# Attention scores of two key groups as 64-row products in the two halves of the array, in three steps per chunk

## The chip, the core and the metric

The kernel runs on one core of one Trainium2 chip. The metric is the device time of one execution in microseconds; the median of several runs is compared. The engines are PE (TensorE, the matrix array, with PEld for its weight loads), DVE (VectorE), ACT (ScalarE), POOL (GpSimd) and SP (SyncE, which issues most DMAs). Matrix products write into PSUM, which has eight banks here: four in a pool `acc` and four in a pool `mx`.

## The reference

One inference step of a decoder of two layers, for a prompt of 512 tokens and 8 samples of 4 new tokens (544 tokens in all, width 1024). A layer is a SwiGLU feed-forward half-step, a mixer and a second half-step; the mixer is four heads of a gated delta rule beside a sliding-window attention with 8 query heads of 64, in two groups that share a key and a value head each. The part that the change touches is the attention of the prompt, in chunks of 128 tokens: every query sees its own chunk and the one before, 128 keys back, with a learned sink in the softmax.

```python
s = jnp.einsum('bnqhgd,bnkhd->bnhgqk', q, k).astype(jnp.float32) * (SWA_HEAD_DIM ** -0.5)
s = jnp.where(allowed[None, :, None, None], s, -jnp.inf)
sink = jnp.broadcast_to(sinks.astype(jnp.float32)[None, None, :, :, None, None], s.shape[:-1] + (1,))
p = jax.nn.softmax(jnp.concatenate([s, sink], axis=-1), axis=-1)[..., :-1]
return jnp.einsum('bnhgqk,bnkhd->bnqhgd', p.astype(v.dtype), v)
```

## The kernel before

Tokens lie along the free dimension and features on the 128 partitions. The dense products (the feed-forwards and the projections into and out of the mixer) are in `mm3`, line 588: every product is three, with weights and activations split into high and low parts (`whi`, `wlo`, `xh`, `xl`), on 256 or 288 tokens at a time, and they write `ps_d` in the pool `acc`. Everything else of the mixer is written as generators, called streams here: `attention`, `sample_attention`, `inverse`, `chain` and others. After each dense product `mm3` calls `pump`, which runs the ready stream of the best rank (`PRIO`) up to its next `yield`. A `yield 0` gives the turn back to the dense products for one product; a `yield` of a number of steps puts the stream to sleep for so many. All streams share the four banks of `mx`, in turn: the next `mx` tile waits until the bank that was taken longest ago is free. SBUF tiles of 128 x 512 come from a pool of 64 slots.

`ORDER` sets the order of the heads' projections in the mixer. At its "|" `drain` pumps the streams without dense products until the transforms of all heads (`T`, `QK`, `VI` in the trace) are there. A scheduler then sets the final order on each engine from the program so written.

The attention's steps on the streams' clock are eight blocks of scores, i = 2n + gg for chunk n and group gg. `sq[hh]` holds the queries of head hh of group 0 in partitions 0 to 63 and of group 1 in 64 to 127; `kfe` holds the keys in the same way. For a product over all 128 rows, the kernel keeps a copy of the keys for each group with zeros in the other half, `kz` (lines 1342 to 1346). `scores(i)` makes four products with the chunk before (`ps_sp`, line 1359, not for n = 0) and four with its own (`ps_sc`, line 1366), each with a `yield 0` behind it, so that dense products come between; ACT copies `ps_sp` into the tile `A`, DVE writes `ps_sc` over it where the mask allows (line 1368), and `softmax` follows on DVE, ACT (the exps, line 1332) and POOL. `turn(i)` transposes the block on PE (`ps_pt`, line 86), and `values(n)` multiplies both groups with the values (`ps_av`, lines 1392 and 1396). `LAG` sets how many blocks lie between them. `sample_attention` uses `kz` once more, for the samples' own keys (`ps_nw`, line 1447).

Of the kernel before, what the change touches and what calls it, by code (L numbers as in the profile page):

```python
# [39 lines left out]
def kernel(  # L40
# [23 lines left out]
    def slot(shape, name, dt=F32):  # L64
        return slot_p.tile(shape, dt, tag="s", name=name)
# [7 lines left out]
    def mx(shape, name):  # L73
        return mx_p.tile(shape, F32, tag="mx", name=name)
# [4 lines left out]
    def bc(ap, axis, n):  # L79
        a = ap.unsqueeze(axis)  # L80
        s = list(a.shape)
        s[axis] = n
        return a.to_broadcast(s)
# [589 lines left out]
    def mixer(l, p, norm, nxt, pre):  # L673
# [663 lines left out]
        def attention():  # L1337
            yield from ready("kv", "sq")
            kfe, vt, sq = W["kfe"], W["vt"], W["sq"]

            oswa.extend(sq)
            kz = [slot([P, NTOK], "kz") for _ in range(2)]
            for gg in range(2):
                gp = slice(64 * gg, 64 * gg + 64)
                pool.memset(kz[gg], 0.0)
                act.copy(out=kz[gg][gp], in_=kfe[gp])
            W["kz"] = kz
            F["kz"] = 1
            W.pop("kfe")
            A, PT = {}, {}  # L1350

            def scores(i):
                n, gg = divmod(i, 2)
                qs = slice(n * P, (n + 1) * P)
                a = slot([P, 4, P], "A")
                if n:
                    ps = mx([P, 4, P], "ps_sp")
                    for hh in range(4):
                        pe.matmul(ps[:, hh], sq[hh][:, qs], kz[gg][:, (n - 1) * P:n * P], start=True, stop=True)  # L1359
                        yield 0  # L1360
                    act.copy(out=a, in_=ps)
                else:
                    pool.memset(a, NEG)
                ps = mx([P, 4, P], "ps_sc")
                for hh in range(4):
                    pe.matmul(ps[:, hh], sq[hh][:, qs], kz[gg][:, qs], start=True, stop=True)  # L1366
                    yield 0
                dve.copy_predicated(out=a, mask=bc(M["lower"].bitcast(U32), 1, 4), data=ps)
                softmax(a, p["sink"][:, 4 * gg:4 * gg + 4])
                A[i] = a  # L1370

            def turn(i):
                n = i // 2
                a = A.pop(i)
                ps = mx([P, 4, P], "ps_pt")
                for hh in range(4):
                    transpose(ps[:, hh], a[:, hh])
                    yield 0
                pc = slot([P, 4, P], "pc")
                dve.tensor_tensor(out=pc, in0=ps, in1=bc(upper, 1, 4), op=ALU.mult)  # L1380
                pp = None
                if n:
                    pp = slot([P, 4, P], "pp")
                    dve.tensor_tensor(out=pp, in0=ps, in1=bc(M["slower"], 1, 4), op=ALU.mult)
                PT[i] = pc, pp

            def values(n):

                po = mx([P, 4, P], "ps_av")
                gs = [(slice(64 * gg, 64 * gg + 64), PT.pop(2 * n + gg)) for gg in range(2)]  # L1390
                for gp, (pc, pp) in gs:
                    pe.matmul(po[gp], vt[:, n, gp], pc, start=True, stop=(n == 0))  # L1392
                    yield 0
                for gp, (pc, pp) in gs:
                    if n:
                        pe.matmul(po[gp], vt[:, n - 1, gp], pp, start=False, stop=True)
                        yield 0
                for hh in range(4):
                    act.copy(out=oswa[hh][:, n * P:(n + 1) * P], in_=po[:, hh])

            la, lb = LAG["turn"], LAG["turn"] + LAG["values"]
            for i in range(8 + lb):
                if 0 <= i - lb and (i - lb) % 2:
                    yield from values((i - lb) // 2)
                if 0 <= i - la < 8:
                    yield from turn(i - la)
                if i < 8:
                    yield from scores(i)
                yield LAG["attn"]
            F["attn"] = 1  # L1410

        def sample_attention():


            yield from ready("kv", "sq", "kz")
            kvs, sq, kz = W["kvs"], W["sq"], W["kz"]
            kct = [slot([P, 4, P], "kct") for _ in range(2)]
            for i in range(2):
                kc = slot([P, 4, P], "kc")
# [24 lines left out]
                act.copy(out=sT[gg].rearrange("p (s c) -> p s c", c=16), in_=ps[:, :, gg])  # L1444
            for gg in range(2):
                ps = mx([P, NS], "ps_nw")
                pe.matmul(ps, qz[:, gg].rearrange("p s c -> p (s c)"), kz[gg][:, NP:NTOK], start=True, stop=True)
                yield 0
                nw = sm("nw", (P, 4, 8), 2)
                dve.tensor_tensor(out=nw, in0=ps.rearrange("p (s t) -> p t s", t=4), in1=bc(M["own_s"], 1, 4), op=ALU.mult)  # L1450
                nk[gg] = sm("nk", (P, 4), 2)
                dve.tensor_reduce(out=nk[gg], in_=nw, axis=AX.X, op=ALU.add)
                yield LAG["t"]
# [252 lines left out]
```

## Time and profile before

| what | value |
|---|---|
| median of 3 runs | 2275.59 us (2273.31 to 2281.57) |
| the profiled execution | 2276.84 us, with a span of 2275.1 us in the trace |
| PE busy | 2245.3 us (99% of the span) |
| PEld busy | 2206.3 us (97%) |
| DVE busy | 1246.7 us (55%) |
| ACT busy | 759.4 us (33%) |
| POOL busy | 258.5 us (11%) |
| mean granted clock of PE | 0.981 of full |

An engine's busy time is the sum of the stretches in which it carries out an instruction; overlapping products count once. A product of two fp32 tiles appears as two passes, so the trace counts twice as many as the program. Successive products overlap in the records, so their period, the difference of two starts, tells what one costs, not its own duration. The granted clock is the share of TensorE's full clock that it was allowed.

### The profile page before, as it was taken

How to read it: one execution, taken by the hardware profiler on the slowest of the kernel's cores; microseconds unless marked ns; L12 is line 12 of the kernel's file. 1: busy time of each engine (PE TensorE's matmuls, PEld its weight loads, DVE VectorE, ACT ScalarE, POOL GpSimd, SP SyncE). 2: the span in 40 equal slices, each digit the busy share in tenths (PEclk: the TensorE clock that was granted, in tenths of full speed). 3: DMA queues.
4: the chain of work that ended last, by engine and by line, in shares of the span. 5: the costliest groups of instructions: out<-in, count | busy, mean ns of one | idle time of the engine just before them, and what ended most of it. 6: DMA issues, size and time to landing. Idle time of an engine off the chain costs nothing.

```text
span 2275.1 us, 41968 instructions
## 1 busy us (share of the span) xinstructions
PE 2245.3 (99%) x17639; PEld 2206.3 (97%) x17639; DVE 1246.7 (55%) x2435; ACT 759.4 (33%) x1479; POOL 258.5 (11%) x356
## 2 busy tenths in 40 slices
PE   8999999999999999999999999999999999999998
PEld 7999999999989999999999999999998999999998
DVE  5535435668658553444554353456776675444346
ACT  4222222444544421222432222234344444222123
POOL 6000000235112000000100000013431120000002
PEclk9999999999989999999999999999997999999999
DMA  4332323452212433323222323234421235223224
GB/s 133 88 90 84 91 86 116 121 127 66 81 64 70 140 103 87 91 84 91 86 85 87 91 84 93 84 116 101 112 76 48 77 88 159 84 87 90 84 84 123
DMA packets 416800, 213.48 MB, mean 94 GB/s; under 512 B 39954, under 2 KB 410898, under 8 KB 416580
## 3 DMA queue, kind: packets, MB, share of 16 engines
q1 hardware_dynamic: 414248, 208.88, 32.2%
q8 instruction: 139, 2.28, 0.4%
q10 hardware_dynamic: 1628, 1.32, 0.2%
q0 software_dynamic: 736, 0.61, 0.1%
q14 instruction: 49, 0.40, 0.1%
HBM read 196.07 MB, written 16.73 MB: 94 GB/s over the span
## 4 chain that ended last, share of the span: by engine, by line
PE 91%; DVE 5%; DMA 1%; ACT 1%; issue 1%; POOL 0%; SPq 0%; DVEq 0%; POOLq 0%; ACTq 0%
PE ps_d L588 83%; DVE wlo L531 1%; DVE xl L312 1%; PE ps_x L1174 1%; PE ps_Z L1005 1%; PE ps_av L1392 1%; PE ps_sc L1366 1%; DVE cacc L825 0%; PE ps_u L1127 0%; PE ps_Y L995 0%; PE ps_sp L1359 0%; DMA raw<-in_ffn_w_gate_dram 0%; PE ps_rb L402 0%; PE ps_Tt L86 0%; DVE x L1596 0%
## 5 line engine op out<-in xcount | busy, mean ns | idle before, releaser
L588 PE MATMUL ps_d<-xl,whi 128*128 128x256 f32 (+1 forms) x3520 | 1029.6, 293 | 2.7 <-DVE xl L312 2.6
L588 PE MATMUL ps_d<-xh,whi 128*128 128x256 f32 (+1 forms) x3520 | 1029.2, 293 | 1.8 <-DVE cin L806 1.6
L588 PE MATMUL ps_d<-xh,wlo 128*128 128x256 f32 (+1 forms) x3520 | 1026.2, 292 | 0.0
L529 ACT CAST whi<-raw 128x1024 fp32r<-128x1024 f32 (+1 forms) x340 | 347.4, 1022 | 1159.4 <-PE ps_d L588 776.5
L588 PEld LDWEIGHTS ps_d<-xh,whi 128*128 128x128 f32 x3520 | 673.1, 191 | 8.8 <-issue 2.9
L588 PEld LDWEIGHTS ps_d<-xl,whi 128*128 128x128 f32 x3520 | 673.2, 191 | 5.4 <-DVE xl L312 3.7
L588 PEld LDWEIGHTS ps_d<-xh,wlo 128*128 128x128 f32 x3520 | 672.7, 191 | 2.6 <-issue 2.4
L531 DVE TENSOR_TENSOR wlo<-raw,whi 128x1024 fp32r<-128x1024 f32 (+1 forms) x340 | 408.1, 1201 | 112.5 <-ACT whi L529 111.3
L588 PE MATMUL ps_d<-hh,wlo 128*128 128x288 f32 (+1 forms) x1408 | 405.1, 289 | 0.0
L588 PE MATMUL ps_d<-hl,whi 128*128 128x288 f32 (+1 forms) x1408 | 405.1, 289 | 0.0
L588 PE MATMUL ps_d<-hh,whi 128*128 128x256 f32 (+1 forms) x1408 | 403.2, 289 | 0.0
L588 PEld LDWEIGHTS ps_d<-hl,whi 128*128 128x128 f32 x1408 | 266.9, 190 | 0.0
L588 PEld LDWEIGHTS ps_d<-hh,wlo 128*128 128x128 f32 x1408 | 266.7, 190 | 0.0
L588 PEld LDWEIGHTS ps_d<-hh,whi 128*128 128x128 f32 x1408 | 265.6, 190 | 0.1
L639 DVE SCALAR_TENSOR_TENSOR x<-ps_d,x 128x256 f32<-128x256 f32 (+1 forms) x192 | 83.3, 439 | 240.5 <-PE ps_d L588 240.1
L608 DVE TENSOR_TENSOR g<-ps_d,rb 128x256 f32<-128x256 f32 (+1 forms) x176 | 77.0, 438 | 235.0 <-PE ps_d L588 215.7
L608 DVE TENSOR_TENSOR u<-ps_d,rb 128x256 f32<-128x256 f32 (+1 forms) x176 | 77.5, 441 | 226.2 <-PE ps_d L588 226.2
L381 POOL TENSOR_TENSOR sq<-sq 128x544 f32<-128x544 f32 x34 | 52.6, 1546 | 1216.9 <-DVE wlo L531 1066.6
L588 PE MATMUL ps_d<-oh,whi 128*128 128x288 f32 (+1 forms) x256 | 73.7, 294 | 1.1 <-DVE x L1596 0.8
L588 PE MATMUL ps_d<-ol,whi 128*128 128x256 f32 (+1 forms) x256 | 74.4, 292 | 0.0
L588 PE MATMUL ps_d<-oh,wlo 128*128 128x256 f32 (+1 forms) x256 | 74.4, 292 | 0.0
L630 ACT CAST hh<-th 128x544 fp32r<-128x544 f32 x88 | 57.0, 647 | 37.2 <-DVE th L627 37.2
(414 smaller groups left out, 2066.2 us busy)
## 6 DMA issues: line engine op xcount, KB each, us to landing
raw<-in_ffn_w_gate_dram SPq DMA_DIRECT2D x88, 512.0 KB
raw<-in_ffn_w_up_dram SPq DMA_DIRECT2D x88, 512.0 KB
raw<-in_ffn_w_down_dram SPq DMA_DIRECT2D x64, 512.0 KB
raw<-in_w_in_dram SPq DMA_DIRECT2D x36, 512.0 KB
raw<-in_ffn_w_down_dram SPq DMA_DIRECT2D x40, 384.0 KB
S<-in_state_gdn_dram SPq DMA_DIRECT2D x32, 256.0 KB
xd<-x SPq DMA_DIRECT2D x16, 272.0 KB
x<-xd SPq DMA_DIRECT2D x16, 272.0 KB
```

The source lines that it names most:

```text
L312: dve.scalar_tensor_tensor(out=lo[:, s], in0=v, scalar=w, in1=h.bitcast(F32)[:, s], op0=ALU.mult, op1=ALU.subtract)
L381: eng.tensor_tensor(out=self.sq, in0=self.sq, in1=s2, op=ALU.add)
L529: act.copy(out=hi[:, 0:kn], in_=v)
L531: dve.tensor_tensor(out=lo[:, 0:kn], in0=v, in1=hi.bitcast(F32)[:, 0:kn], op=ALU.subtract)
L588: pe.matmul(ps, a[:, k], b, start=(k == 0 and a is hi and b is rh), stop=(k == kn - 1 and a is lo))
L608: when(norm, lambda: dve.tensor_tensor(out=dst[:, o:o + n], in0=ps, in1=norm.rb[:, o:o + n], op=ALU.mult))
L630: act.copy(out=a, in_=th)
L639: dve.scalar_tensor_tensor(out=xv, in0=ps, scalar=0.25, in1=xv, op0=ALU.mult, op1=ALU.add)
L1005: pe.matmul(ps[:, q], Tt[q // 4][:, q % 4], Y[:, q], start=True, stop=True)
L1174: pe.matmul(ps[:, :, r0:r0 + 4], ss[s // 4][:, s % 4], kqs[:, :, 32 * h + r0:32 * h + r0 + 4], start=True, stop=True)
L1366: pe.matmul(ps[:, hh], sq[hh][:, qs], kz[gg][:, qs], start=True, stop=True)
L1392: pe.matmul(po[gp], vt[:, n, gp], pc, start=True, stop=(n == 0))
```

## The change

The scores of both groups of a chunk are made in one step. The zero-padded keys are gone: each product reads 64 partitions of `sq` and of `kfe`, group 0 in the upper half of the array's rows, group 1 in the lower, in turn, into a bank for each group and part: `ps_sp` and `ps_sc` take all four banks of `mx` at once. There is no `yield` between the products. The loop has three steps a chunk (values of chunk n − 2, scores of chunk n, turns of chunk n − 1) with a sleep of `LAG["attn"]` behind each, in place of one block for each of 8 + 4 steps. `kfe` is kept to the end of the attention, and the samples' own keys are read from it.

```diff
--- before.py
+++ after.py
@@ -1339,35 +1339,29 @@
             kfe, vt, sq = W["kfe"], W["vt"], W["sq"]
 
             oswa.extend(sq)
-            kz = [slot([P, NTOK], "kz") for _ in range(2)]
-            for gg in range(2):
-                gp = slice(64 * gg, 64 * gg + 64)
-                pool.memset(kz[gg], 0.0)
-                act.copy(out=kz[gg][gp], in_=kfe[gp])
-            W["kz"] = kz
-            F["kz"] = 1
-            W.pop("kfe")
             A, PT = {}, {}
 
-            def scores(i):
-                n, gg = divmod(i, 2)
+            def scores(n):
+
                 qs = slice(n * P, (n + 1) * P)
-                a = slot([P, 4, P], "A")
-                if n:
-                    ps = mx([P, 4, P], "ps_sp")
+                parts = ("ps_sp", "ps_sc") if n else ("ps_sc",)
+                ps = {(name, gg): mx([P, 4, P], name) for name in parts for gg in range(2)}
+                for name in parts:
+                    ks = slice(qs.start - P, qs.start) if name == "ps_sp" else qs
                     for hh in range(4):
-                        pe.matmul(ps[:, hh], sq[hh][:, qs], kz[gg][:, (n - 1) * P:n * P], start=True, stop=True)
-                        yield 0
-                    act.copy(out=a, in_=ps)
-                else:
-                    pool.memset(a, NEG)
-                ps = mx([P, 4, P], "ps_sc")
-                for hh in range(4):
-                    pe.matmul(ps[:, hh], sq[hh][:, qs], kz[gg][:, qs], start=True, stop=True)
-                    yield 0
-                dve.copy_predicated(out=a, mask=bc(M["lower"].bitcast(U32), 1, 4), data=ps)
-                softmax(a, p["sink"][:, 4 * gg:4 * gg + 4])
-                A[i] = a
+                        for gg in range(2):
+                            gp = slice(64 * gg, 64 * gg + 64)
+                            pe.matmul(ps[name, gg][:, hh], sq[hh][gp, qs], kfe[gp, ks], start=True, stop=True)
+                for gg in range(2):
+                    a = slot([P, 4, P], "A")
+                    if n:
+                        act.copy(out=a, in_=ps["ps_sp", gg])
+                    else:
+                        pool.memset(a, NEG)
+                    dve.copy_predicated(out=a, mask=bc(M["lower"].bitcast(U32), 1, 4), data=ps["ps_sc", gg])
+                    softmax(a, p["sink"][:, 4 * gg:4 * gg + 4])
+                    A[2 * n + gg] = a
+                yield 0
 
             def turn(i):
                 n = i // 2
@@ -1398,22 +1392,25 @@
                 for hh in range(4):
                     act.copy(out=oswa[hh][:, n * P:(n + 1) * P], in_=po[:, hh])
 
-            la, lb = LAG["turn"], LAG["turn"] + LAG["values"]
-            for i in range(8 + lb):
-                if 0 <= i - lb and (i - lb) % 2:
-                    yield from values((i - lb) // 2)
-                if 0 <= i - la < 8:
-                    yield from turn(i - la)
-                if i < 8:
-                    yield from scores(i)
-                yield LAG["attn"]
+            for n in range(6):
+                if n >= 2:
+                    yield from values(n - 2)
+                    yield LAG["attn"]
+                if n < 4:
+                    yield from scores(n)
+                    yield LAG["attn"]
+                if 1 <= n < 5:
+                    for gg in range(2):
+                        yield from turn(2 * n - 2 + gg)
+                    yield LAG["attn"]
+            W.pop("kfe")
             F["attn"] = 1
 
         def sample_attention():
 
 
-            yield from ready("kv", "sq", "kz")
-            kvs, sq, kz = W["kvs"], W["sq"], W["kz"]
+            yield from ready("kv", "sq")
+            kvs, sq, kfe = W["kvs"], W["sq"], W["kfe"]
             kct = [slot([P, 4, P], "kct") for _ in range(2)]
             for i in range(2):
                 kc = slot([P, 4, P], "kc")
@@ -1444,7 +1441,7 @@
                 act.copy(out=sT[gg].rearrange("p (s c) -> p s c", c=16), in_=ps[:, :, gg])
             for gg in range(2):
                 ps = mx([P, NS], "ps_nw")
-                pe.matmul(ps, qz[:, gg].rearrange("p s c -> p (s c)"), kz[gg][:, NP:NTOK], start=True, stop=True)
+                pe.matmul(ps, qz[:, gg].rearrange("p s c -> p (s c)"), kfe[:, NP:NTOK], start=True, stop=True)
                 yield 0
                 nw = sm("nw", (P, 4, 8), 2)
                 dve.tensor_tensor(out=nw, in0=ps.rearrange("p (s t) -> p t s", t=4), in1=bc(M["own_s"], 1, 4), op=ALU.mult)
```

The scheduler's order shows what becomes of it. The first place is the scores of chunk 2 in the first layer, on PE. Before (one block of chunk 2; the next block looks alike):

```order
L1359 MATMUL ps_sp<-kz,sqt 128x128
L588 MATMUL ps_d<-xh,whi 128x256
L1359 MATMUL ps_sp<-kz,sqt 128x128
L588 MATMUL ps_d<-xl,whi 128x256
L1359 MATMUL ps_sp<-kz,sqt 128x128
L588 MATMUL ps_d<-xh,wlo 128x256
L1359 MATMUL ps_sp<-kz,sqt 128x128
L588 MATMUL ps_d<-xh,whi 128x256
L1366 MATMUL ps_sc<-kz,sqt 128x128
L588 MATMUL ps_d<-xl,whi 128x256
L1366 MATMUL ps_sc<-kz,sqt 128x128
L588 MATMUL ps_d<-xh,wlo 128x256
```

After, the end of the same chunk's 16 products, behind eight `ps_sp` in turn between the groups (`ps_sp_6074` and `ps_sc_6076` are group 1, `ps_sc_6075` is group 0):

```order
L1354 MATMUL ps_sp_6074<-kfe_5096,sqt_5592 128x128
L588 MATMUL ps_d_6067<-xh_4303,wlo_5867 128x288
L1354 MATMUL ps_sc_6075<-kfe_5096,sqt_5345 128x128
L1354 MATMUL ps_sc_6075<-kfe_5096,sqt_5474 128x128
L1354 MATMUL ps_sc_6075<-kfe_5096,sqt_5533 128x128
L1354 MATMUL ps_sc_6075<-kfe_5096,sqt_5592 128x128
L588 MATMUL ps_d_6067<-xh_4359,whi_5866 128x288
L588 MATMUL ps_d_6067<-xl_4360,whi_5866 128x288
L588 MATMUL ps_d_6067<-xh_4359,wlo_5867 128x288
L1354 MATMUL ps_sc_6076<-kfe_5096,sqt_5345 128x128
L1354 MATMUL ps_sc_6076<-kfe_5096,sqt_5474 128x128
L1354 MATMUL ps_sc_6076<-kfe_5096,sqt_5533 128x128
```

Single products between dense ones have become runs; the two groups' `ps_sp` stand in turn, but their `ps_sc` stand apart, four of group 0 and four of group 1, with dense products between.

The second place is the scores of chunk 3, the last, on PE. Before, the last block's scores (of group 1) stand in the drain, each part in a run, with the products of the delta rule around them:

```order
L1392 MATMUL ps_av<-pc,vt 64x512 x2
L1396 MATMUL ps_av<-pp,vt 64x512 x2
L86 MATMUL ps_pt<-ident,A 128x128 x4
L1359 MATMUL ps_sp<-kz,sqt 128x128 x4
L1366 MATMUL ps_sc<-kz,sqt 128x128 x4
L1174 MATMUL ps_x_6919<-kqs,S_6540 128x2x4 x4
L1174 MATMUL ps_x_6919<-kqs,S_6542 128x2x4 x4
```

After, both groups' scores of chunk 3 stand ahead of the drain, among dense products (`ps_sp_6700` is group 0, `ps_sp_6701` group 1; the first 12 of 29 rows that go on in this way):

```order
L1354 MATMUL ps_sp_6700<-kfe_5096,sqt_5345 128x128
L588 MATMUL ps_d_7209<-xl_4304,whi_6660 128x256
L588 MATMUL ps_d_7209<-xh_4303,wlo_6661 128x256
L1354 MATMUL ps_sp_6700<-kfe_5096,sqt_5474 128x128
L588 MATMUL ps_d_7209<-xh_4359,whi_6660 128x256
L588 MATMUL ps_d_7209<-xl_4360,whi_6660 128x256
L1354 MATMUL ps_sp_6701<-kfe_5096,sqt_5345 128x128
L1354 MATMUL ps_sp_6701<-kfe_5096,sqt_5474 128x128
L1354 MATMUL ps_sp_6700<-kfe_5096,sqt_5533 128x128
L588 MATMUL ps_d_7209<-xh_4359,wlo_6661 128x256
L1354 MATMUL ps_sp_6701<-kfe_5096,sqt_5533 128x128
L588 MATMUL ps_d_7209<-xh_4415,whi_6660 128x256
```

The 16 products of this chunk are no longer in runs: 12 pieces of one to three products, with one or two dense ones between.

The third place is the end of the drain in the first layer, on PE (`ps_Z` belongs to the inverse, `ps_x` and `ps_u` to the samples' delta rule). Before:

```order
L1042 MATMUL ps_Z<-Tt,Y 64x64 x6
L86 MATMUL ps_n_7193<-ident,NT_7133 128x128
L86 MATMUL ps_pt<-ident,A 128x128 x4
L1174 MATMUL ps_x_7215<-kqs,S_7055 128x2x4 x4
L1174 MATMUL ps_x_7215<-kqs,S_7057 128x2x4 x4
L1174 MATMUL ps_x_7252<-kqs,S_7059 128x2x4 x2
L1127 MATMUL ps_u<-VI,Tt 128x128 x4
L1174 MATMUL ps_x_7252<-kqs,S_7059 128x2x4 x2
L1174 MATMUL ps_x_7252<-kqs,S_7061 128x2x4 x4
L1222 MATMUL ps_y_7319<-T_7196,NT_7133 128x128
L1392 MATMUL ps_av<-pc,vt 64x512 x2
L1396 MATMUL ps_av<-pp,vt 64x512 x2
```

After:

```order
L86 MATMUL ps_kd<-ident,kf 128x128 x4
L1042 MATMUL ps_Z<-Tt,Y 64x64 x6
L86 MATMUL ps_n_7216<-ident,NT_7158 128x128
L1174 MATMUL ps_x_7236<-kqs,S_7084 128x2x4 x4
L1174 MATMUL ps_x_7236<-kqs,S_7086 128x2x4 x4
L588 MATMUL ps_d<-xh,whi 128x256
L588 MATMUL ps_d<-xl,whi 128x256
```

Behind the last `ps_Z` the transposes of `A`, half of the `ps_x` and the last `ps_av` are gone from the drain's end; they stand earlier, or among later dense products.

## Rows read from the trace of the kernel before

**Rows 1.** Page, part 1: busy us, share of the span, instructions.

```profile
PE 2245.3 (99%) x17639; PEld 2206.3 (97%) x17639; DVE 1246.7 (55%) x2435; ACT 759.4 (33%) x1479; POOL 258.5 (11%) x356
```

**Rows 2.** Windows: length, busy us of each engine, clock, DMA share, GB/s.

```profile
500.00:530.00 30.00, 30.00 (x250) 30.00 (x250) 23.38 (x70) 13.13 (x41) 10.31 (x18) 1.00 0.45 106
530.00:560.00 30.00, 30.00 (x224) 29.96 (x223) 27.83 (x59) 14.65 (x42) 15.78 (x16) 0.86 0.27 72
```

**Rows 3.** Tile view of kz: duration min/median/max in ns, first and last start.

```profile
L1366 PE MATMUL ps_sc<-kz,sqt x128: 270/275/275, 504.9 to 1729.3; 128*128 128x128 f32 x128
...
L1359 PE MATMUL ps_sp<-kz,sqt x96: 271/275/275, 514.8 to 1728.4; 128*128 128x128 f32 x96
...
L1345 POOL MEMSET kz<- x4: 541/548/550, 494.8 to 1612.3; 128x544 f32 x4
L1346 ACT COPY kz<-kfe x4: 642/643/644, 499.0 to 1615.3; 64x544 f32<-64x544 f32 x4
```

**Rows 4.** Timeline of PE, four scores in a row: start, us, operation.

```profile
504.78 0.28 PE L588 MATMUL ps_d<-xh,whi 128*128 128x256 f32 x1
504.90 1.06 PE L1366 MATMUL ps_sc<-kz,sqt 128*128 128x128 f32 x8
505.71 0.36 PE L588 MATMUL ps_d<-xl,whi 128*128 128x256 f32 x1
505.91 0.28 PE L588 MATMUL ps_d<-xh,wlo 128*128 128x256 f32 x1
```

**Rows 5.** Timeline of PE, single scores between dense products.

```profile
509.33 0.30 PE L588 MATMUL ps_d<-xh,wlo 128*128 128x288 f32 x1
509.46 0.38 PE L1366 MATMUL ps_sc<-kz,sqt 128*128 128x128 f32 x2
...
509.82 0.38 PE L1366 MATMUL ps_sc<-kz,sqt 128*128 128x128 f32 x2
```

**Rows 6.** Timeline of PE, four products of 32 rows.

```profile
751.99 0.29 PE L588 MATMUL ps_d<-xh,wlo 128*128 128x288 f32 x1
752.21 1.14 PE L1283 MATMUL ps_s<-um,kds 32*128 32x512 f32 x8
753.28 0.38 PE L588 MATMUL ps_d<-xh,whi 128*128 128x256 f32 x1
753.50 0.28 PE L588 MATMUL ps_d<-xl,whi 128*128 128x256 f32 x1
```

**Rows 7.** Timeline of PE, visits of 24 rows between dense products.

```profile
424.38 0.42 PE L86 MATMUL ps_cst<-ident,cst 24*128 24x24 f32 x4
424.74 0.39 PE L588 MATMUL ps_d<-xl,whi 128*128 128x256 f32 x1
425.05 0.42 PE L86 MATMUL ps_cst<-ident,cst 24*128 24x24 f32 x4
```

**Rows 8.** Windows: two stretches at half clock, columns as in rows 2.

```profile
637.20:650.90 13.70, 13.70 (x62) 11.20 (x60) 6.28 (x18) 1.94 (x8) 0.00 (x0) 0.50 0.00 1
...
1753.40:1770.40 17.00, 17.00 (x81) 14.04 (x79) 7.12 (x20) 2.25 (x9) 0.00 (x0) 0.50 0.00 1
```

**Rows 9.** Timeline of PE, the end of the first layer's drain.

```profile
638.02 1.06 PE L86 MATMUL ps_pt<-ident,A 128*128 128x128 f32 x4
638.88 4.28 PE L1174 MATMUL ps_x<-kqs,S 128*128 128x8 f32 x20
...
644.85 2.57 PE L1174 MATMUL ps_x<-kqs,S 128*128 128x8 f32 x12
```

**Rows 10.** Waits of PE, 613 to 652: us, times, longest.

```profile
PE ps_t L86 <- DVE E L932: 1.7, 1, 1.7
PE ps_Tt L86 <- DVE kds L1190: 0.8, 1, 0.8
PE ps_pt L86 <- DVE rs_a L858: 0.5, 1, 0.5
```

**Rows 11.** Tile view of A: the exp of the softmax, columns as rows 3.

```profile
L1332 ACT ACTIVATE A<-A,snm x64: 384/387/404, 509.5 to 1734.3; 128x128 f32<-128x128 f32 x64
```

## The prediction

> **What bounds the kernel now.** I read the page's busy times first, then the stretch of the attention by windows, then single stretches of the timeline on PE, and last the waits. The page says that PE is busy for 2245.3 of 2275.1 us and DVE for 1246.7 [rows 1], so only time on PE's own line counts: a product saved, a clock granted, or a wait made. The windows show the same in the stretch where the scores run in the first layer: PE 30.00 of 30.00 us in both halves, with DVE at 23.38 and then 27.83 [rows 2]. The reader is to keep both: PE has no slack to win back, and DVE, which does the softmax, has little left. The profiled execution took 2276.84 us, 1.25 above the median of 2275.59; I sum on the former and give the forecast against the latter.
>
> **What the scores cost today.** The tile view counts 128 + 96 passes on PE [rows 3]. A product is two passes in this trace, so these are 112 products, 56 in each layer. Before the change they stand in two ways. Four in a row start at 504.90 and the next dense product at 505.71; against the 0.12 us period of dense products, the next one is also late (505.71 to 505.91, 0.20) [rows 4]: (505.91 − 0.12) − 504.90 = 0.89 us, 0.22 for a product. Single ones between dense products repeat every 509.82 − 509.46 = 0.36 us, of which the dense one is 0.13 [rows 5]: 0.225 for a product. Both ways agree, so mixing full-height products with dense ones costs nothing here, and a layer's scores cost 56 × 0.223 = 12.5 us.
>
> **What they cost after.** Still 56 products, but of 64 rows. Two things decide: do two in different halves run together, and what does PE lose where it goes over from 128 rows to fewer and back? The kernel before has no 64-row product among dense ones. The nearest row is the four 32-row products of 512 columns, in four row quarters: they start at 752.21 after a dense product at 751.99, and the second dense product behind them starts at 753.50 [rows 6]. Taking off a dense period on either side, they hold PE for (753.50 − 0.12) − (751.99 + 0.13) = 1.26 us. One such product has four times the columns of a score product, so by 0.22 us it takes 0.86 to 0.89 by itself; four one after the other would be 3.4. So the quarters did run together, and about 0.40 us is left for going in and coming back. A second place agrees: visits of 24 rows with one dense product between repeat every 425.05 − 424.38 = 0.67 us [rows 7], which less a dense period is 0.54 for four very short passes. I take 0.40 for each visit, from a row with fewer rows per tile than 64. The bounds are 0 and 0.54, and two halves side by side count as one product's time, with the bound that they don't overlap at all.
>
> The Trainium skill (TensorE: Matmul & The Clock Gate, Part 3, Measured speedup vs the span model) has 3.07 times for four row tiles of this size. By it those four would take 3.44 / 3.07 = 1.12 us and a visit 0.26, and the sum below would be 34 × 0.14 = 4.8 us lower; the row has 2.7 times, and the measurement decides.
>
> Now the order. It has 17 visits in a layer, the same in both.
> - Chunk 0: 8 products in 4 pairs, one visit: 0.89 + 0.40 = 1.29 us.
> - Chunk 1: 16 in one visit. The first 8 are in pairs, the others stand g0 g0 g1 g1 g0 g1 g0 g1, five product times: 0.89 + 1.11 + 0.40 = 2.40.
> - Chunk 2: 8 in pairs, then one dense product, then four of group 0, then three dense ones, then four of group 1. The last eight have nothing beside them: three visits, 0.89 × 3 + 1.20 = 3.87.
> - Chunk 3: scattered in 12 visits of 1 to 3 products with 13 dense products between; only three pairs are left, so 13 product times: 2.90 + 12 × 0.40 = 7.70.
>
> Together 15.26 against 12.5, **+2.8 us** in a layer, **+5.5** in both. The gain of pairing in chunks 0 to 2 is eaten by chunk 3. Bounds: visits for nothing, 8.46 a layer, −8.1 in both; no overlap, 19.3 a layer, +13.6; visits at 0.54, +4.8 on top of the forecast.
>
> **What leaves other engines.** Two memsets and two copies a layer (548 and 643 ns) [rows 3] leave POOL and ACT. They end before the first score, under dense products on PE, and neither engine is full [rows 2]. I cost them at nothing; if their cover were gone, the two copies would be 1.3 us a layer.
>
> **What moves: the end of the drain.** The drain at the "|" has no dense work. Its last piece before the change runs at a granted clock of 0.50, that is 1.2 of 2.4 GHz, for 13.70 us in the first layer and 17.00 in the second, with PE busy all the time [rows 8], so up to half of it, 15.4 us, is there to be won. In it stand the last four transposes of A (638.02), 20 and 12 passes of ps_x (638.88, 644.85) and the last ps_av [rows 9]. The three-step order ends the attention earlier: behind the last ps_Z there remain ps_n and eight ps_x products, 16 of the 32 passes, and no transposes of A and no ps_av. What has gone ahead still has to run somewhere: among dense products at full clock, or beside the earlier ps_Z and ps_x, where the trace shows 0.50 too. I take about 3 us a layer, **−6**, between 0 and −15.4.
>
> **What moves: waits.** PE waits 1.7 + 0.8 + 0.5 = 3.0 us in the drain of the first layer, most of it for DVE [rows 10]. With the last softmax done earlier, DVE comes to the drain with less before it: I take **−2** in both layers, between 0 and −6.
>
> **What is added: a wait for banks.** A burst asks for all four banks of the pool mx at once, and the next stream's tile waits until the copies, the predicated copies and so the softmax before them are through. Each softmax has four exps of 387 ns on ACT [rows 11], so two of them hold ACT 8 × 0.387 = 3.1 us, and the copy of the second group's ps_sp can stand behind the first four. The products of other streams stand in PE's order, and dense products behind them. The trace of before has hardly a wait for a bank in the attention, so its price is bounded by 0 and 3.1 us for each of three chunks and two layers, 18.6. In the order, 26 dense products (3.1 us) stand between chunk 1's burst and the next tile of the pool, a cached-key transpose, and the first ps_pt follows after three more, so by then the ACT copy that frees the second bank may be under way or not; behind chunk 2's products the gap is far longer. I take half of 3.1 for one chunk a layer: **+3**.
>
> **Sum.** 5.5 − 6 − 2 + 3 = +0.5 us on 2276.84, so 2277.3; less the 1.25 by which that execution lies above the median, 2276. By what a measurement of this kernel can tell (0.5%, 11.4 us) that is no change.
>
> **The rivals**, each with the other terms as they are and taken against the median.
> - B, visits cost nothing. For it: mixing of 128-row products costs nothing [rows 4, 5]. Against it: the 0.40 and 0.54 of [rows 6, 7]. Then −8.1 in place of +5.5: 2276 − 13.6 = 2262. The Trainium skill's span model for packed tiles (same page and section) has no term for going in and out, and would have it so. 0.13.
> - C, halves don't overlap, because two passes of a product and their weight loads alternate. The four quarters speak against it [rows 6]. Then +13.6 in place of +5.5: 2276 + 8.1 = 2284. 0.10.
> - D, the other side: the clock falls in chunk 3's scatter, as it did where short products fill PE [rows 8]. Chunk 3 with its dense products is about 7.7 + 13 × 0.12 = 9.3 us at full clock; at half in both layers, +18.6: 2295. It decides from about 6 us lost in a layer on (2287 − 2276 = 11, over two). Against it: dense products stand between all visits. 0.10.
> - E, also slower: PE waits for banks at the upper end, 18.6 in place of 3: 2292. For it: DVE at 27.83 of 30 [rows 2], through which every block's reduce has to go before ACT can start its exps. 0.07. The Trainium skill (TensorEngine Tiling (Array Packing), Restrictions and Gotchas, Gotcha 1: PSUM Pressure) says that row tiles need different banks, which is why the burst takes four.
> - My forecast: 0.60.
>
> **How the numbers follow.** The time is that of my forecast. Its own range, by the bounds of the drain's clock and waits (−15.4 and −6, or nothing), is 2263 to 2284; B and C lie at these ends. The range given goes a little past both, 2260 to 2291: that leaves out the part of B in which the clock gives more as well, and most of D and E, some 0.17 in all. Faster by over 0.5% means under 2264: most of B and the edge of the forecast, 0.14. Slower means over 2287: D and E, 0.17. Within: 0.69.
>
> **What the profile after would show.** Pairs: alternating products of a burst start two at a time, a burst of eight holds PE 1.3 us. Visits: a single score between dense products costs 0.6 rather than 0.22. Clock: the stretch at 0.50 before the drain's end is 10 us or less. Banks: no wait of PE on A or snm in the attention above 1 us. The forecast is wrong if a visit costs under 0.1 or over 0.8 us, if the stretches at 0.50 grow by over 20 us in all, or if PE's busy share in the attention falls under 97%.

## The result, and the profile after

The changed kernel takes 2297.27 us (median of 4, 2294.65 to 2301.18) against 2274.45 us (median of 4). The ratio on record is 1.0109, with a 95% interval from 1.0081 to 1.0137 (the quotient of the two medians is 1.0100). That is slower by twice the 0.5% that a measurement of this kernel can tell. The forecast was 2276 with a range up to 2291.

The profiled execution took 2299.23 us, with a span of 2297.5, 22.4 more than before. The page's first part, which answers to [rows 1]:

```profile
PE 2255.9 (98%) x17639; PEld 2204.3 (96%) x17639; DVE 1244.5 (54%) x2435; ACT 755.7 (33%) x1475; POOL 252.5 (11%) x352
```

PE is busy for 10.6 us more, of 22.4: so about half of the loss is work at a slower pace, and half is PE standing still (41.6 us of the span, 29.8 before).

**The products.** The timeline of PE in the changed kernel at the scores of chunk 0, which answers to [rows 4] (start, length, operation, passes):

```profile
504.25 0.28 PE L588 MATMUL ps_d<-xh,whi 128*128 128x256 f32 x1
504.46 1.16 PE L1354 MATMUL ps_sc<-kfe,sqt 64*128 64x128 f32 x16
505.55 0.39 PE L588 MATMUL ps_d<-xl,whi 128*128 128x256 f32 x1
505.77 0.28 PE L588 MATMUL ps_d<-xh,wlo 128*128 128x256 f32 x1
```

(505.77 − 0.12) − (504.25 + 0.12) = 1.28 us for eight products; 1.29 was forecast. The two halves do run together: in chunk 2, four products of one group alone, with nothing beside them, take as long.

```profile
532.76 0.29 PE L588 MATMUL ps_d<-xh,wlo 128*128 128x288 f32 x1
532.98 1.16 PE L1354 MATMUL ps_sc<-kfe,sqt 64*128 64x128 f32 x8
534.06 0.40 PE L588 MATMUL ps_d<-xh,whi 128*128 128x288 f32 x1
534.30 0.30 PE L588 MATMUL ps_d<-xl,whi 128*128 128x288 f32 x1
```

(534.30 − 0.13) − (532.76 + 0.13) = 1.28 again. The scatter of chunk 3, the first row being the dense product behind a group of three scores:

```profile
593.04 0.39 PE L588 MATMUL ps_d<-xh,wlo 128*128 128x256 f32 x1
593.36 0.49 PE L1354 MATMUL ps_sp<-kfe,sqt 64*128 64x128 f32 x2
593.77 0.39 PE L588 MATMUL ps_d<-xh,whi 128*128 128x256 f32 x1
594.09 0.48 PE L1354 MATMUL ps_sp<-kfe,sqt 64*128 64x128 f32 x2
```

A visit with one dense product repeats every 594.09 − 593.36 = 0.73 us; less a dense period of 0.12 and a product of 0.22, the price of going in and out is 0.39. So these rows bear out the term of the scores.

The Trainium skill (TensorE: Matmul & The Clock Gate, Part 3, Measured speedup vs the span model) has a pack of tiles cost one product and about 4 ns for each further tile; by an estimate from that rule the burst of eight would hold PE for some 0.9 us. The trace has 1.28: the pairs agree, the passage in and out is not in the rule, and the measurement decides.

**The waits.** The longest waits of PE in the mixer of the first layer and of the second (us, times, longest); they answer to [rows 10]:

```profile
PE ps_ds L1135 <- DVE u L1131: 3.6, 1, 3.6
PE ps_Z L1005 <- ACT ptn L1477: 2.9, 1, 2.9
```

```profile
PE ps_ds L1135 <- DVE u L1131: 3.6, 1, 3.6
PE ps_Z L1005 <- ACT ptn L1477: 1.9, 1, 1.9
```

Neither wait has a counterpart before, where the longest is 1.7 us in the first layer [rows 10]. In the second layer PE's waits before, from 1616.5 to 1843.8 us, are these:

```profile
PE ps_g L1193 <- ACT tsq L883: 0.9, 1, 0.9
PE ps_Tt L86 <- DVE kds L1190: 0.6, 1, 0.6
PE ps_d L588 <- DVE x L1596: 0.4, 1, 0.4
PE ps_ot L86 <- DVE o L1058: 0.4, 1, 0.4
```

The first of the two is a place in DVE's order. DVE and PE there:

```profile
676.54 0.35 DVE L1247 TENSOR_SCALAR u<-ps_u,bkn 128x128 f32<-128x128 f32 x1 [5.11 <-PE ps_u L1244]
676.81 4.43 DVE L1514 SCALAR_TENSOR_TENSOR sqt<-sqt,par,rb 128x544 f32<-128x544 f32 x4
681.16 1.11 DVE L1131 TENSOR_SCALAR u<-ps_u,bkn 128x128 f32<-128x128 f32 x4
```

```profile
681.65 0.46 PE L1135 MATMUL ps_ds<-u,kd 128*128 128x128 f32 x2 [3.64 <-DVE u L1131]
```

The four scalings of the attention's output (`sqt`, 4.4 us together) now stand ahead of the four `u` of the delta rule's chain, for which PE waits with `ps_ds`, and dense products stand behind that. Before the change the four `u` came first and the scalings 5.6 us later:

```profile
664.89 1.13 DVE L1131 TENSOR_SCALAR u<-ps_u,bkn 128x128 f32<-128x128 f32 x4 [0.28 <-PE ps_u L1127]
...
670.46 0.77 DVE L1517 SCALAR_TENSOR_TENSOR sqt<-sqt,par,rb 128x544 f32<-128x544 f32 x1
```

The second wait is for a bank. ACT, PE and DVE there:

```profile
570.05 0.68 ACT L828 ACTIVATE cacb<-cacc 128x568 f32<-128x568 f32 x1 [0.92 <-DVE cacc L825]
570.63 0.25 ACT L1476 COPY pts<-ps_ps 128x128 f32<-128x128 f32 x1
570.78 0.25 ACT L1477 COPY ptn<-ps_ps 32x128 f32<-32x128 f32 x1
...
571.09 0.25 ACT L1477 COPY ptn<-ps_ps 32x128 f32<-32x128 f32 x1
```

```profile
557.63 0.60 PE L86 MATMUL ps_pt<-ident,A 128*128 128x128 f32 x4
558.21 0.60 PE L86 MATMUL ps_pt<-ident,A 128*128 128x128 f32 x4
...
563.33 0.27 PE L86 MATMUL ps_ps<-ident,As 128*128 128x128 f32 x1
...
565.43 0.27 PE L86 MATMUL ps_ps<-ident,As 128*128 128x128 f32 x1
...
567.89 0.29 PE L588 MATMUL ps_d<-xh,wlo 128*128 128x288 f32 x1
571.08 5.47 PE L1005 MATMUL ps_Z<-Y,Tt 128*128 128x16 f32 x32 [2.90 <-ACT ptn L1477]
576.48 1.98 PE L1386 MATMUL ps_av<-pc,vt 128*64 128x512 f32 x4
```

```profile
572.32 0.68 DVE L1378 TENSOR_TENSOR pp<-ps_pt,slower 128x512 f32<-128x512 f32 x1
...
573.51 0.68 DVE L1378 TENSOR_TENSOR pp<-ps_pt,slower 128x512 f32<-128x512 f32 x1
```

The inverse's `ps_Z` needs a bank of `mx`. Its four are held by the two `ps_pt` of a step, one for each group, and by the two `ps_ps` of the samples. DVE frees the former with `pp`, which it starts at 572.32 and 573.51. The copies that free the latter stand on ACT behind an activation (line 828) that waits for the convolution, and `ps_Z` is the next in PE's order, so PE stands still for 2.9 us. It starts when the first `ptn` is through (570.78 + 0.25), though both `ps_pt` were written before that `ps_ps`: what it takes here is the bank that comes free first, and not, as was said of the pool above, the one that was taken longest ago.

**The clock.** The longest windows of the changed kernel at half clock: in the first layer the run of short products behind that wait, a stretch that begins in the scatter of chunk 3, and the drain; in the second layer the run again and the drain (columns as in [rows 2]; the third and the fifth answer to [rows 8]):

```profile
572.80:579.60 6.80, 6.80 (x27) 4.41 (x26) 5.04 (x11) 0.00 (x0) 0.21 (x1) 0.50 0.28 78
596.70:606.90 10.20, 10.20 (x39) 8.41 (x37) 3.10 (x10) 1.40 (x3) 1.38 (x1) 0.50 0.00 0
630.80:641.00 10.20, 9.70 (x37) 6.23 (x36) 5.65 (x20) 2.55 (x14) 0.56 (x1) 0.50 0.11 34
1699.20:1716.30 17.10, 17.10 (x70) 13.57 (x70) 7.85 (x15) 3.70 (x16) 2.28 (x8) 0.50 0.11 31
1760.60:1767.40 6.80, 6.38 (x31) 5.97 (x30) 3.58 (x8) 1.96 (x12) 0.00 (x0) 0.50 0.24 72
```

The drain's end has 10.2 and 6.8 us in place of 13.70 and 17.00, about as forecast. But the run of `ps_Z`, `ps_av` and `ps_avs` is now at 0.50 too, and so is the end of the scatter (596.7 to 606.9 us in the first layer, 1729.9 to 1736.8 in the second). The scores end some 5 and 3 us into these two stretches; the rest of them is dense products. Visits with one dense product between, inside the first:

```profile
598.44 0.79 PE L1354 MATMUL ps_sc<-kfe,sqt 64*128 64x128 f32 x2
599.17 0.58 PE L588 MATMUL ps_d<-xh,whi 128*128 128x256 f32 x1
599.68 0.80 PE L1354 MATMUL ps_sc<-kfe,sqt 64*128 64x128 f32 x4
```

599.68 − 598.44 = 1.24 us from visit to visit, where it was 0.73.

**The account.** Taken between the same dense products in both traces (498.0 to 721.7 us before and 498.2 to 732.9 after; 1616.5 to 1843.8 and 1627.7 to 1866.0), with the waits of PE summed and half of the time at 0.50 counted as lost, which is an estimate that takes PE to be at work all that time:

| | longer | waits of PE | half of the time at 0.50 | what is left |
|---|---|---|---|---|
| first layer | +11.1 | 3.6 to 8.7: +5.1 | 27.3 to 34.1: +3.4 | +2.6 |
| second layer | +11.0 | 2.3 to 8.1: +5.8 | 37.5 to 44.4: +3.4 | +1.8 |

What is left, by subtraction, is about the size that the visits were to have (+2.8).

### The profile page after: what moved, and what is told of

The parts are those of the page before. It is cut to its first block, busy times and chain, and to the rows that moved or that the text cites. A ratio compares the mean times of both kernels' runs of the same rounds, so it can differ in the third digit from the quotient of the medians.

```text
span 2297.5 us, 42003 instructions
## 1 busy us (share of the span) xinstructions
PE 2255.9 (98%) x17639; PEld 2204.3 (96%) x17639; DVE 1244.5 (54%) x2435; ACT 755.7 (33%) x1475; POOL 252.5 (11%) x352
## 4 chain that ended last, share of the span: by engine, by line
PE 91%; DVE 5%; DMA 1%; issue 1%; ACT 1%; POOL 0%; SPq 0%; DVEq 0%; POOLq 0%
PE ps_d L588 82%; DVE wlo L531 1%; PE ps_Z L1005 1%; DVE xl L312 1%; PE ps_sc L1354 1%; PE ps_av L1386 1%; PE ps_Y L995 0%; PE ps_x L1174 0%; PE ps_sp L1354 0%; PE ps_av L1390 0%; PE ps_rb L402 0%; DMA raw<-in_ffn_w_gate_dram 0%; PE ps_Tt L86 0%; DVE sqt L1514 0%; DMA xtok<-in_x_prompt_dram 0%
```

## The experiments

Theory W: the new steps moved work into waits and into stretches at half clock, and 64 rows by themselves cost only the visits. Theory M: going over to 64 rows and back, with the clock that falls on it, is the cost. Two more came up on the way: P (pace: with fewer steps the attention runs ahead of the rest) and B (banks: both groups' transposes are held at once). Each run is compared with the kernel before on the same chip; e1 to e4, e5 to e8 and e9 to e12 ran on three chips, and the changed kernel stands in none of these groups. A difference to the changed kernel therefore goes by the ratios, whose intervals together leave about 8 us open: by time alone, e1, e3 to e7 and e11 are not told apart from the changed kernel, while e2, e8, e9, e10 and e12 are. Since every execution comes with its mean granted clock, the time splits in two, as an estimate: time × (1 − clock) is lost to the clock, and the other part is what the program would take at full clock. A clock is given to 0.001, which is 2.3 us.

| run | median us | ratio to before (95%) | lost to the clock | at full clock |
|---|---|---|---|---|
| before | 2270.1 | | 34 | 2236 |
| changed | 2297.3 | 1.0109 (1.0081 to 1.0137) | 46 | 2251 |
| e1, steps with 128 rows | 2293.9 | 1.0094 (1.0072 to 1.0117) | 39 | 2254 |
| e2, old steps with 64 rows | 2321.0 | 1.0216 (1.0190 to 1.0241) | 60 | 2261 |
| e3, scaling later | 2292.1 | 1.0089 (1.0068 to 1.0109) | 42 | 2250 |
| e4, chunk 3 in runs | 2290.0 | 1.0073 (1.0049 to 1.0097) | 39 | 2250 |
| e5, copies on DVE | 2293.5 | 1.0100 (1.0078 to 1.0123) | 39 | 2255 |
| e6, e3 to e5 together | 2289.0 | 1.0072 (1.0047 to 1.0098) | 42 | 2247 |
| e7, slower steps | 2289.1 | 1.0080 (1.0058 to 1.0102) | 50 | 2238 |
| e8, old loop, runs | 2268.0 | 0.9992 (0.9975 to 1.0009) | 25 | 2245 |
| e9, e8 with scaling later | 2264.9 | 0.9971 (0.9954 to 0.9989) | 28 | 2238 |
| e10, e8 with 64 rows | 2306.9 | 1.0156 (1.0129 to 1.0183) | 48 | 2261 |
| e11, e7 with 128 rows | 2297.4 | 1.0111 (1.0083 to 1.0138) | 53 | 2245 |
| e12, turns apart | 2273.3 | 1.0005 (0.9986 to 1.0025) | 48 | 2226 |

(Medians of each column. For before, the 23 executions beside e9 to e12; the 11 beside e1 to e4 had 2273.5, 39 and 2235, the 17 beside e5 to e8 2270.3, 34 and 2236. The ratios are those on record, not quotients of the medians.)

**e1: the new steps with 128-row products.**

```diff
-    pe.matmul(ps[name, gg][:, hh], sq[hh][gp, qs], kfe[gp, ks], start=True, stop=True)
+    pe.matmul(ps[name, gg][:, hh], sq[hh][:, qs], kz[gg][:, ks], start=True, stop=True)
```

(`kz` is made as before the change.)

> The changed kernel with its three steps a chunk and its runs of products, but with the zero-padded keys kept and every score a 128-row product. The order on PE is the same to within a few rows, with the same runs and the same scatter in chunk 3. Theory W (the new steps moved work into two waits of PE, 3.6 and 2.9 us in the first layer, and into stretches at half clock; 64 rows cost only about 0.40 us a visit, 3 us a layer): about 6 us less than the changed kernel, 2291, with both waits still there and the half clock about as long. Theory M (going over to 64 rows and back is what costs, by itself and by the clock that falls in the scatter): back to the kernel before, 2272 to 2278. Theory C: no half clock in the scatter of chunk 3, since full products keep PE busy, so 10 us or more less than the changed kernel.

2293.9: M falls as the main cause. With no 64-row score left, 20 of the 23 us are still there, and both waits with them (3.6 for `u`, 4.3 for `ptn` in the first layer). Theory C is half right: the scatter (597.4 to 602.4 and 1726.2 to 1731.2 us) is at full clock, but the run behind `ps_Z` in the first layer is at half clock for 20.5 us in place of 6.8, and the 10 us are not won.

**e2: the old steps with 64-row products.**

```diff
-    pe.matmul(ps[:, hh], sq[hh][:, qs], kz[gg][:, qs], start=True, stop=True)
+    pe.matmul(ps[:, hh], sq[hh][64 * gg:64 * gg + 64, qs], kfe[64 * gg:64 * gg + 64, qs], start=True, stop=True)
```

(and so for `ps_sp`.)

> The kernel before with its twelve steps and its yields, but without zero-padded keys and with 64-row products: 36 single products between dense ones and 3 runs in a layer, none beside one of the other group. Theory W: 39 visits at 0.40 us and 56 products at 0.22, so 15.6 us a layer more than before, 2274 + 31 = 2305, with no wait for ptn or u. Theory M: the same or more, 2305 to 2325. If visits cost nothing, 2274.

2321.0, more than W's 2305. At full clock it is 26 us above the 2235 of before in its group; 31 were expected, so the price of a visit holds (a little high). The rest, 60 us lost to the clock in place of 34 to 39, was not in W: many single visits lower the clock. In that, M has a part of the truth.

**e3: the scaling later.**

```diff
             on.sums()
-            yield LAG["ss"]
+            yield LAG["ss"] + 15
```

> The changed kernel with the sleep ahead of the spread of the attention's norm 15 steps longer, so that on DVE the four scalings of the attention's output stand behind the four u of the chain, as they did before the change. Theory W: PE's wait of 3.6 us for u goes in both layers, 7 us less, about 2290. Theory M: the wait has nothing to do with it and comes back elsewhere, 2295 to 2299.

2292.1, near the 2290 of W, but within the noise of the changed kernel. The wait for `u` is gone from the trace; in its place PE waits 1.6 and 1.3 us for the casts of the scaled tiles, which are late now. At full clock nothing is won (2250, with 2251 in the changed kernel), so this run does not show what the wait for `u` is worth.

**e4: chunk 3 in runs.**

```diff
+                with (tc.high_priority(offset=300) if n == 3 else nullcontext()):
                     for name in parts:
                     ...
```

> The changed kernel with the scores of chunk 3 given a higher rank in the scheduler, so that they stand in two runs (twelve and four products) in place of twelve visits; groups are not paired in them. Theory W with the price of 0.40 us: 10 visits less in a layer, 4.0 us, less 3 products' times of pairing, 0.7: 3.3 us a layer, 2291; if the half clock in the scatter goes as well, up to 5 us a layer more, 2281. Theory M in its strong form (the visits and their clock are all of the 23 us): 2278.

2290.0, 7 us less, at the edge of the noise, all of it clock (46 to 39). At full clock nothing is won, although the visits are fewer: PE's waits in the first layer rose from 8.7 to 12.1 us.

**e5: the copies on DVE.**

```diff
-                act.copy(out=ptn[:, :, gg], in_=ps[0:NS, 1].rearrange("p (s c) -> p s c", c=16))
+                dve.tensor_copy(out=ptn[:, :, gg], in_=ps[0:NS, 1].rearrange("p (s c) -> p s c", c=16))
```

(and so for `pts`.)

> The changed kernel with the four copies of the samples' transposed weights (pts and ptn, which free the bank that ps_Z waits for) made by DVE in place of ACT, where they stand behind an activation that waits for the convolution on POOL and DVE. Theory W: PE's wait of 2.9 and 1.9 us for ptn goes, 5 us less than the changed kernel, about 2292; the run of short products behind it (ps_Z, ps_av, ps_avs) stays as it is, so no more than that. Rival: the wait is not the cost, the next operand is late as well, 2297.

2293.5; by the trace the rival is right. PE's waits in the first layer:

```profile
PE ps_Z L1005 <- DVE pp L1378: 5.2, 1, 5.2
PE ps_ds L1135 <- DVE u L1131: 3.6, 1, 3.6
```

The same `ps_Z` waits 5.2 us, longer than before the edit, now for `pp`: that is what frees the banks of the two `ps_pt`. On DVE the copies of `ptn` stand behind `pc` and `pp`, so a `ps_pt` is now the first of the four to come free; in the changed kernel it was a `ps_ps`. So all four banks are held while `ps_Z` waits.

**e6: e3, e4 and e5 together.**

> The changed kernel with the three single edits together: copies on DVE, the scaling 15 steps later, and the scores of chunk 3 in runs. Theory W, by the sums measured so far: 2297 less 5 (scaling), 7 (runs) and 5 (copies): 2280. If the places share one cost (all of them gain the same half clock), 2287 or more.

2289.0: not the sum of the three (2280), but the other forecast, 2287 or more. The wait of `ps_Z` for `pp` is there with 5.2 us as in e5, and the run of short products behind it is at half clock for 20.5 us.

**e7: a longer sleep.** `attn` in `LAG` is 36 in place of 28.

> The changed kernel with the attention's sleep 36 in place of 28 steps, nothing else. In the order, the scores of chunk 3 then stand in the drain in one run, as before the change, chunk 1 has all its products in pairs, the scalings stand behind the four u, and the run of ps_Z, ps_av and ps_avs loses its ps_av. Theory P (pace: without a step for every product the attention runs ahead of the rest of the mixer, and that is what makes the waits and the scatter): most of the loss is gone, 2272 to 2280, and PE doesn't wait for u. Theory M (64 rows): 2290 or more. If the waits of PE come from the four banks held at once, the wait for ptn stays: 2285 to 2290.

2289.1. At full clock most of the loss is gone (2238, with 2236 before), the waits for `u` and `ptn` with it; but 50 us are lost to the clock. P was right on the waits and not on the time.

**e8: the old loop with runs of 128-row products.**

```diff
                     for hh in range(4):
                         pe.matmul(ps[:, hh], sq[hh][:, qs], kz[gg][:, (n - 1) * P:n * P], start=True, stop=True)
-                        yield 0
...
-                    yield 0
+                yield 0
```

> The kernel before with its twelve steps, zero-padded keys and 128-row products, one group at a time, but no yield between the products of a block, so that eight products stand in a run. No bank is held longer and no product has 64 rows. Theory P: the attention takes some 100 steps fewer, runs ahead as in the changed kernel, the scaling comes ahead of u in DVE's order, and the kernel loses 10 to 20 us, 2284 to 2294, with a wait of 3 to 4 us for u in each layer. Rival (the merging of both groups into one step with four banks at once is what costs): as before, 2270 to 2278.

2268.0, as before: P falls as the main cause of the time. At full clock it is not out: the attention runs ahead here too, and the scalings stand ahead of `u`, for 2.5 us of waiting in each layer. That kernel takes 9 us more at full clock, where the changed one has 15, and 9 us less are lost to the clock.

**e9: e8 with the scaling later** (the edit of e3).

> The kernel of the old loop with runs of 128-row products (2268 us) with the sleep ahead of the spread of the attention's norm 15 steps longer, so that the scalings stand behind the four u on DVE. If PE's wait for u (2.5 us a layer in that kernel) and its wait for z (2.4) come from the four scalings: up to 10 us less, 2258 to 2263, faster than the kernel before. If they come back at the next operand: 2266 to 2270.

2264.9, between the two forecasts: 0.29% less than before, clear of zero by its interval, though under the 0.5% that a measurement of this kernel can tell. The wait for `u` is gone; 1.3 and 1.2 us for the casts stay. At full clock it is some 6 us under e8 (2244.5 to 2238.3).

```profile
PE ps_d L588 <- ACT oh L1502: 1.3, 1, 1.3
PE ps_d L588 <- DVE ol L1503: 1.2, 1, 1.2
```

**e10: e8 with 64-row products** (the edit of e2).

> The old loop with runs, one group at a time, but with 64-row products from the keys themselves in place of 128-row ones. No pairs. In the first layer 15 visits in place of as many runs. Price of 0.40 us for a visit: 6 us a layer, 12 in all at full clock, 2280; the scatter of the last block (7 visits) may lower the clock on top, up to 5 us. If a visit costs nothing in a run: 2268.

2306.9, 39 us above e8 where 12 were expected. At full clock it is 16, which is some 0.5 us for each of the 30 visits; the last block, whose products stand singly, has seven of a layer's 15. The other 23 are clock: 48 lost in place of 25. So where 64-row products find no partner, the clock cost more here than the visits.

**e11: e7 with 128-row products**, the same order of products on PE.

> The three steps with a sleep of 36, as in the run before, but with zero-padded keys and 128-row products: the order on PE is the same product for product (4 products of chunk 0 aside). What pairing saves, by the burst of eight at 1.28 us against 1.78 for eight in a row: 0.5 in chunk 0, 1.4 in chunk 1, nothing in chunk 2, 0.5 in chunk 3, 2.4 us a layer; so 5 us more than 2289, about 2294. If pairing gains nothing: 2289.

2297.4: 8 us more by the medians, 7 by the ratios with some 8 us of noise, and 6.5 at full clock. That fits the 5 us that pairing was expected to gain, and is not clear of zero.

**e12: the turns apart.**

```diff
                     for gg in range(2):
                         yield from turn(2 * n - 2 + gg)
-                    yield LAG["attn"]
+                        yield LAG["attn"]
```

> The changed kernel with a sleep between the transposes of the two groups, so that a step holds one bank for them and not two. In the order the scores of chunk 3 stand in one run in the drain, and the scalings behind eight u. Theory B (PE's wait at ps_Z is for banks that both groups' transposes and the samples' transposes hold at once): no wait of PE for ptn or pp above 1 us, and with the waits and the scatter gone 2275 to 2285. If the wait comes from the lateness of DVE and ACT themselves, it stays at 2 us or more.

2273.3, 24 us less than the changed kernel and no different from before. No wait for `ptn`, `pp` or `u` is left; the longest that there are:

```profile
PE ps_s L1111 <- DVE S L1139: 1.9, 1, 1.9
PE ps_sp L1354 <- DVE rs_a L858: 0.5, 1, 0.5
```

At full clock it is the fastest of all, 10 us under before; the clock takes it back (48 lost, 34 before). The edit slows the attention as well: it sleeps 4 × 28 = 112 steps a chunk, where the changed kernel has 84 and e7 3 × 36 = 108. In e7 the two turns stand together, and it has no wait for `ptn` or `u` either; in both traces no `ps_pt` stands near that `ps_Z` any more (the last ones ahead of it end at 522.8 in e12 and 522.2 in e7, `ps_Z` starts at 567.5 and 564.9). So the end of the wait at `ps_Z` does not tell B from P. At about the same pace e12 takes 12 us less than e7 at full clock, which speaks for turns that are apart; what of it is banks isn't shown.

## Why the prediction was wrong

- **What they cost after (+5.5): right.** 1.28 and 0.39 us were measured for 1.29 and 0.40, and what is left in the account is 2.6 + 1.8 = 4.4 us. The 0.40 was taken from products of 32 rows in four quarters; that it would hold for 64 rows in two halves was assumed, and it did.
- **What moves: waits (−2): the step that failed.** I took DVE's load in the drain as what moves, and did not follow the attention's end to what comes behind it. The stage after it, the norm and its scalings, moved ahead of the chain's `u` in DVE's order, and `ps_Z` behind a bank. Measured: +5.1 and +5.8, 10.9 in place of −2. e1 has both waits without a 64-row score; e3 and e9 show that the wait for `u` comes from the scalings' place, e7 and e12 that both waits go when the attention is slower.
- **What is added: a wait for banks (+3): wrong place.** The bursts never waited. The banks that mattered are those of the two groups' transposes, held together since a step makes both turns. I had priced the scores' four banks and not the turns' two. e5 shows that they are held until `pp`; that holding both at once is the cause, and not the attention's pace, isn't shown, since e12 changes both. The Trainium skill (TensorEngine Tiling (Array Packing), Restrictions and Gotchas, Gotcha 1: PSUM Pressure) speaks of banks for the tiles that run together; here they came free in time, and the trace shows the shortage a stage later.
- **The end of the drain (−6): right where it stood, and given back, the other step that failed.** By the windows the drains gained (13.7 − 10.2 + 17.0 − 6.8) / 2, some 6.8 us, but the scatter and the run behind `ps_Z` went to half clock, so that over both layers the clock cost 3.4 + 3.4 = +6.8 in place of −6. The sum had no term for half clock ahead of the drain; what went ahead was taken to run among dense products at full clock or beside products at 0.50 already, and the scatter stood in rival D alone.
- The forecast's sum was +0.5; measured by its own terms it is 4.4 + 6.8 + 10.9 = 22.1, and the span grew by 22.4. So the clock was 12.8 us off and the waits, with the banks, 9.9. Rival D had the scatter's clock: the two stretches that begin in it, 10.2 and 6.8 us at 0.50, lose 8.5 of its 18.6 us. Rival E had a wait for banks, at another place. The prediction's rivals B (a visit costs 0.39, not nothing) and C (eight in pairs take as long as four alone) are out.
- None of the signs by which the forecast would have called itself wrong came: a visit costs 0.39 us, the stretches at 0.50 grew by 13.7 us in the two mixers, and PE is busy for 97.3% of 498.2 to 607.0 us, where the scores run. They looked at the scores, and not at what stands behind them.

What stays open: whether the bank or the attention's pace makes the wait at `ps_Z`; and the mean granted clock differs between executions of one kernel (0.978 to 0.983 in the changed one) with one trace of each, so the clock's part is known as medians, and place by place for single executions alone. That e12's gain at full clock could be kept with a better clock wasn't tried.

## What to carry to other kernels

When an edit ends one stream earlier, follow its successor: read in each engine's order what the next stage now stands ahead of, and which buffers of a shared pool two groups hold at the same time. Merging two halves of the work into one step doubles what the step holds; a sleep between the halves, which also slowed the stream, was worth more here (24 us) than the faster products (some 7 in e11, within the noise). And split a time into what the clock takes and what is left before judging an edit: e8 and e12 look like nothing, and each is two effects of 10 us that cancel.

## What was not expected of the hardware

- Where products of 64 rows stand without a partner, in runs of four and eight and in the singles of the last block, the granted clock fell for longer: e10 lost 48 us to it and e8, with 128 rows in the same loop, 25 (medians).
- Going to 64-row products and back costs 0.39 us each time at full clock, for a burst of eight in pairs as for four in one half or a single one.
